# Inverting the triangular blocks of two recurrent layers: to and from the inverter by copies and 32x32 transpositions on chip in place of DRAM transfers

## The chip, the cores and the metric

The kernel runs on one core of a Trainium2 chip. A core has TensorE (PE, matrix products), VectorE (DVE), ScalarE (ACT), GpSimd (POOL) and SyncE (SP), which here issues the DMA transfers. Each engine works through its own queue of instructions in order; engines wait for each other by semaphores. The metric is the device time of one launch in microseconds, as a median over runs.

## The reference

A trunk of four residual layers on one sequence of 256 positions and width 1024, in float32. Layers 0 and 3 mix the positions with RWKV-7, layer 1 with stick-breaking attention, layer 2 with a sparse attention over 64 selected keys; a SwiGLU network follows each. What the change touches is the RWKV mixer, cut to its recurrence:

```python
def step(state, inp):                      # state: 64 x 64 per head, 16 heads
    r_t, w_t, k_t, v_t, kk_t, a_t = inp
    sa = jnp.einsum('bhvk,bhk->bhv', state, kk_t)
    state = (state * w_t[:, :, None, :]
             - sa[..., None] * (kk_t * a_t)[:, :, None, :]
             + v_t[..., None] * k_t[:, :, None, :])
    return state, jnp.einsum('bhvk,bhk->bhv', state, r_t)
_, y = lax.scan(step, s0, (r, decay, k, v, kk, a))
...                                        # norm of y per head, plus (sum r*k*r_k) * v
out = (y * g) @ w_out                      # g: the gate
```

## The kernel before, in words

The 256 positions are cut into four chunks of 64. Within a chunk the recurrence is solved at once: the scores of a chunk form a strictly triangular 64x64 matrix per head, and the inverse of (one plus that matrix) is applied to the chunk's vectors. 16 heads and 4 chunks make 64 such matrices. From chunk to chunk a 64x64 state per head is passed on.

One RWKV layer runs through these steps; the names are those of the profile. Products for keys, values, receptance and gates come first. Then PE makes the scores ("sc"), and DVE multiplies them by a mask into "SB" (16 operations of 128x512 per layer; SB holds the triangular matrices). The 32x32 blocks on the diagonal, two for each of the 64 matrices, lie in four groups of 32 partitions. They are inverted all at once by DVE: the tile "inv" gives each of the 128 blocks a partition of its own, its first half (`ab_`) the block and its second half (`XI`) the inverse, which begins as the identity. 31 steps follow, each of them a product into "xtmp" and a subtraction into "inv"; step i works on (i + 1) rows of (31 − i) elements.

The inverted blocks go to "XT" in the layout that the products want. `combine` then fills XT's off-diagonal blocks, for two of the eight head pairs at a time: DVE transposes XT into "xd", PE makes 32x32 products ("cmb"), which are copied to "zs", PE makes a second set of products, and the result goes to XT. After that the recurrence over the chunks can start: products "pS", "xu", "qu", "Sn" and "Y", each small, each needing what came before it.

How the blocks get from SB to inv and from inv to XT, before: on the chip's DRAM. Eight DMAs write SB's blocks to "scr" in another order of axes, one DMA reads scr into `ab_`, and one loads the identity into `XI`. After the 31 steps one DMA writes `XI` to "scx" and eight DMAs read it back into XT. All are issued on SP's queue, which also loads the weights ("raw").

Meanwhile PE has other work from the same layer that the recurrence does not wait for at once: the value products ("vp", and in layer 3 "pv"), transpositions "qct", "vtok", the products "bv" (SB with the values), the sums "bn" and the gate products "pg". A bn takes its operand from DVE ("prs", split into high and low parts as "prhl", by a CAST and a subtraction), and its result goes through DVE again ("pr"). A pg takes the gate weights' high part "wh" (a cast, on ACT or DVE), low part "wl" (a subtraction on DVE), and the rest of them as "wy" (made on DVE).

The order on each engine is not that of the code. A class `Plan` records all operations, and a list scheduler with its own table of costs and ranks places them on the engines before the program is built; operations of the queue `anye` go to ACT or DVE as it decides. It repeats this 16 times (ROUNDS) and once more with a table `NUDGES`, whose entries shift the ranks of ranges of operations by pseudo-random amounts. Where PE would have nothing to do it puts in dummy bf16 products ("warm_o", L1831 before). All other instructions are emitted from one line (L780 before, L765 after), so the profile's groups are told apart by names. The delay that the scheduler reckons with for a DMA has an extra part, `op.lag`.

Of the kernel before, what the change touches and what calls it, by code (L numbers as in the profile page):

```python
# [28 lines left out]
NCH = S // C  # L29
# [159 lines left out]
class Queue:  # L189
# [152 lines left out]
class Plan:  # L342
# [37 lines left out]
    def record(self, eng, method, args, kw):  # L380
# [22 lines left out]
        if "dma" in method and isinstance(args[0], View):  # L403
            op.lands = args[0].buf.kind == "dram"
            op.lag = 900.0 if args[0].buf.group == "raw" else 0.0
# [378 lines left out]
def trunk(ctx: ExitStack, tc: tile.TileContext, xT_in, vecs_in, wts, lora_in, consts_in, id32_in, nqk_in, outT, order, layers=None):  # L784
# [11 lines left out]
    def T(shape, group=None, name="t", dtype=F32):  # L796
        return plan.tile(sb, [P] + list(shape), dtype, group, name)
# [273 lines left out]
    def rwkv(j, layer, after):  # L1071
# [208 lines left out]
        scr = plan.tile(dram, [4, 32, 32, 32], F32, None, f"scr{j}", "dram")  # L1280
        for g in range(4):
            b = g % 2
            for k in range(2):
                sp.dma_start(scr[g][16 * k:16 * k + 16].rearrange("u i t -> i u t"),
                             SB[k][g * 32:(g + 1) * 32, g // 2, :, :, 0, b * 32:(b + 1) * 32].rearrange("p a c t -> p (a c) t"))
        inv = T([2, 32, 32], "s7", "inv")
        ab_, XI = inv[:, 0], inv[:, 1]
        sp.dma_start(ab_, scr.rearrange("g u i t -> (g u) i t"))
        sp.dma_start(XI, id32_in)
        xtmp = T([S], "xtmp", "xtmp")  # L1290
        for i in range(31):
            t = xtmp[:, :(i + 1) * (31 - i)].rearrange("p (a b) -> p a b", a=i + 1)
            a = ab_[:, i:i + 1, i + 1:].to_broadcast([P, i + 1, 31 - i])
# [700 lines left out]
```

## Time and profile before

| what | us |
|---|---|
| median of three runs (lowest, highest) | 1399.46 (1389.28, 1410.45) |
| the profiled execution, its own time | 1401.71 |
| its span in the trace | 1399.9 |
| PE, DVE, ACT busy in it | 1384.5, 1113.9, 750.4 |
| mean granted clock of PE, share of full | 0.991 |

1.8 us of the profiled execution lie around its span. The profile's times count from the span's start. A row of the timeline or the chain gives the start, the length, the engine, the operation with output<-input, and in brackets the idle time of the engine before it with what ended it; a row for a group gives total busy time and the mean of one in ns. The granted clock is the share of TensorE's full clock that the chip allowed in a window. Rows of ACT and DVE overlap slightly where one instruction starts before the last has drained.

### The profile page before, as it was taken

The numbers are of one execution on the slowest core, as the hardware profiler recorded it, in microseconds if no ns is written. First come the engines' busy times: TensorE is split into PE (matmuls) and PEld (weight loads), VectorE is DVE, ScalarE is ACT, GpSimd is POOL, SyncE is SP. The second block draws the span as 40 slices with busy tenths as digits, with TensorE's granted clock in tenths as the row PEclk, the third lists the DMA queues.
The fourth block names the chain that finished last, engine by engine and source line by source line (L and its number), as shares of the span: only waits on it lengthen the run. The fifth ranks groups of instructions, "written<-read, shape, count | busy, mean of one in ns | idle before, by whom it ended". The sixth has DMA issues, their size and how long they took to land.

```text
span 1399.9 us, 25594 instructions
## 1 busy us (share of the span) xinstructions
PE 1384.5 (99%) x10204; PEld 1195.1 (85%) x10204; DVE 1113.9 (80%) x1960; ACT 750.4 (54%) x1280; POOL 8.0 (1%) x16
## 2 busy tenths in 40 slices
PE   8999999999999999999999999999999999999998
PEld 7888898888888898888887798888878878988887
DVE  7988598887667779896689888986499875988864
ACT  4755675444456755354466864444349256744532
POOL 0000000000000000000000000000000000000000
PEclk9999899999999999999999999999999989999999
DMA  7344155555555355665655445555543440555563
GB/s 254 102 129 140 33 152 184 191 188 189 183 180 158 119 154 192 184 194 183 210 165 151 158 153 181 193 183 189 155 136 110 117 139 20 166 190 186 181 191 126
DMA packets 78231, 224.26 MB, mean 160 GB/s; under 512 B 23712, under 2 KB 24224, under 8 KB 77856
## 3 DMA queue, kind: packets, MB, share of 16 engines
q1 hardware_dynamic: 78112, 222.63, 50.6%
q8 instruction: 80, 1.31, 0.4%
q14 instruction: 39, 0.32, 0.1%
HBM read 219.46 MB, written 3.15 MB: 159 GB/s over the span
## 4 chain that ended last, share of the span: by engine, by line
PE 93%; DVE 3%; DMA 2%; SPq 1%; ACT 0%; issue 0%; DVEq 0%
PE gate L780 18%; PE up L780 18%; PE dn L780 18%; PE po L780 7%; PE rp L780 3%; PE qk L780 3%; PE kp L780 3%; PE vps L780 3%; PE vp L780 2%; PE z L780 2%; PE q L780 2%; PE k L780 2%; PE Y L780 1%; PE sc L780 1%; DMA raw<-in_wts_dram 1%; PE cmb L780 1%
## 5 line engine op out<-in xcount | busy, mean ns | idle before, releaser
L780 ACT CAST wh<-raw 128x1024 fp32r<-128x1024 f32 x329 | 344.6, 1051 | 364.2 <-PE dn L780 112.6
L780 DVE TENSOR_TENSOR wl<-raw,wh 128x1024 fp32r<-128x1024 f32 x375 | 453.2, 1221 | 80.4 <-ACT wh L780 72.9
L780 PE MATMUL up<-xg,wh 128*128 128x512 f32 x704 | 255.3, 397 | 0.0
L780 PE MATMUL gate<-xg,wh 128*128 128x512 f32 x704 | 254.3, 396 | 0.0
L780 PE MATMUL dn<-h,wh 128*128 128x512 f32 x704 | 247.1, 395 | 0.0
L780 PE MATMUL up<-xg,wl 128*128 128x256 f32 x704 | 197.5, 280 | 0.0
L780 PE MATMUL gate<-xg,wl 128*128 128x256 f32 x704 | 197.4, 280 | 0.0
L780 PE MATMUL dn<-h,wl 128*128 128x256 f32 x704 | 197.2, 280 | 0.0
L780 PEld LDWEIGHTS gate<-xg,wh 128*128 128x128 f32 x704 | 132.0, 188 | 31.2
L780 PEld LDWEIGHTS up<-xg,wh 128*128 128x128 f32 x704 | 132.0, 188 | 31.0
L780 PEld LDWEIGHTS dn<-h,wh 128*128 128x128 f32 x704 | 132.0, 188 | 30.9
L780 PEld LDWEIGHTS up<-xg,wl 128*128 128x128 f32 x704 | 133.0, 189 | 0.2
L780 PEld LDWEIGHTS gate<-xg,wl 128*128 128x128 f32 x704 | 133.0, 189 | 0.1
L780 PEld LDWEIGHTS dn<-h,wl 128*128 128x128 f32 x704 | 133.0, 189 | 0.0
L780 DVE TENSOR_TENSOR gus<-gus,rstd 128x512 f32<-128x512 f32 x88 | 59.6, 686 | 0.8
L780 PE MATMUL vp<-xv,raw 128*128 128x256 f32 x256 | 58.3, 384 | 0.0
L780 PEld LDWEIGHTS vp<-xv,raw 128*128 128x128 f32 x256 | 47.6, 190 | 8.0 <-issue 0.7
L780 PE MATMUL rp<-prx,wh 128*128 128x256 f32 x256 | 51.2, 299 | 0.0
L780 DVE TENSOR_TENSOR xt<-xt,dn 128x256 f32<-128x256 f32 x64 | 26.8, 418 | 30.3 <-PE dn L780 29.7
L780 PE MATMUL po<-yhl,wh 128*128 128x256 f32 x256 | 49.4, 293 | 0.0
L780 PE MATMUL po<-ohl,wh 128*128 128x256 f32 x256 | 48.4, 289 | 0.0
L780 PE MATMUL qk<-xg,wh 128*128 128x512 f32 x128 | 46.4, 403 | 0.0
(318 smaller groups left out, 2385.0 us busy)
## 6 DMA issues: line engine op xcount, KB each, us to landing
raw<-in_wts_dram SPq DMA_DIRECT2D x401, 512.0 KB, 3.7
lora<-in_lora_dram SPq DMA_DIRECT2D x2, 1280.0 KB, 9.8
xt<-in_xT_dram SPq DMA_DIRECT2D x4, 256.0 KB, 3.7
lora<-in_lora_dram SPq DMA_DIRECT2D x2, 512.0 KB, 6.2
scr<-SB SPq DMA_DIRECT2D x16, 64.0 KB, 1.9
inv<-in_id_dram SPq DMA_DIRECT2D x2, 512.0 KB, 3.7
inv<-scr SPq DMA_DIRECT2D x2, 512.0 KB, 4.6
scx<-inv SPq DMA_DIRECT2D x2, 512.0 KB, 3.4
```

Source lines behind the costliest of these rows:

```text
L780: getattr(getattr(nc, o.eng), method)(*map(real, args), **{k: real(a) for k, a in kw.items()})
```

## The change

Four edits.

One: the way in. Eight copies (queue `anye`, 32 partitions x 512 elements each) put SB's blocks into a tile "blocks" with axes [row t, k, a, c], and one DVE transposition of all 32x32 blocks, 128x1024, writes `inv[:, 0]`. The identity is still loaded by DMA. Two: because a 32x32 transposition leaves the axes of a partition the other way round, the views `ab_` and `XI` on inv are rearranged from [i, t] storage to [t, i] storage: what was the inner axis of a step's operands, one float from the next, now goes 32 floats from one element to the next, and what was the outer axis is now contiguous. The 31 steps are otherwise the same. Three: the way out. A second transposition of 128x1024 goes from `inv[:, 1]` to another "blocks" tile, and eight copies from there fill XT. The 18 DMAs per layer through scr and scx are gone. Four: `op.lag` becomes 2500 for a DMA into a part of a tile on chip that is not contiguous (900 remains for "raw"), and NUDGES is a new table; both change the order of the whole program.

```diff
 NUDGES = [[
-    (424148, 5631, 5681, 1000), (179145, 5680, 5980, 1000), (140712, 6286, 6406, 1000), (48283, 6712, 6762, 8000),
...
+    (441210, 581, 589, 3000), (474839, 1087, 1387, 1000), (64567, 1455, 1505, 300), (132794, 641, 649, 1000),
...
-            op.lag = 900.0 if args[0].buf.group == "raw" else 0.0
+            wide = not op.lands and args[0].region().mask is not None
+            op.lag = 900.0 if args[0].buf.group == "raw" else 2500.0 if wide else 0.0
...
-        scr = plan.tile(dram, [4, 32, 32, 32], F32, None, f"scr{j}", "dram")
-        for g in range(4):
-            b = g % 2
-            for k in range(2):
-                sp.dma_start(scr[g][16 * k:16 * k + 16].rearrange("u i t -> i u t"),
-                             SB[k][g * 32:(g + 1) * 32, g // 2, :, :, 0, b * 32:(b + 1) * 32].rearrange("p a c t -> p (a c) t"))
+        ct_ = T([32, 2, 4, NCH], "blocks", "blocks")
+        for k in range(2):
+            for g in range(4):
+                r, b = slice(g * 32, (g + 1) * 32), g % 2
+                anye.copy(ct_[r, :, k].rearrange("p t a c -> p a c t"), SB[k][r, g // 2, :, :, 0, b * 32:(b + 1) * 32])
         inv = T([2, 32, 32], "s7", "inv")
-        ab_, XI = inv[:, 0], inv[:, 1]
-        sp.dma_start(ab_, scr.rearrange("g u i t -> (g u) i t"))
-        sp.dma_start(XI, id32_in)
+        dve.transpose(flat(inv[:, 0]), ct_.rearrange("p t k a c -> p (t k a c)"))
+        sp.dma_start(inv[:, 1], id32_in)
+        ab_, XI = [inv[:, i].rearrange("p t i -> p i t") for i in range(2)]
         xtmp = T([S], "xtmp", "xtmp")
         for i in range(31):
             t = xtmp[:, :(i + 1) * (31 - i)].rearrange("p (a b) -> p a b", a=i + 1)
             a = ab_[:, i:i + 1, i + 1:].to_broadcast([P, i + 1, 31 - i])
             b = XI[:, :i + 1, i:i + 1].to_broadcast([P, i + 1, 31 - i])
             dve.tensor_tensor(t, a, b, op=ALU.mult)
             dve.tensor_tensor(XI[:, :i + 1, i + 1:], XI[:, :i + 1, i + 1:], t, op=ALU.subtract)
-        scx = plan.tile(dram, [4, 32, 32, 32], F32, None, f"scx{j}", "dram")
-
         XT = [T([16, C], t, "XT") for t in ("wh", "wl")]
         for k in range(2):
             anye.memset(XT[k], 0.0)
-        sp.dma_start(scx.rearrange("g u i t -> (g u) i t"), XI)
+        ct_ = T([32, 2, 16], "blocks", "blocks")
+        dve.transpose(ct_.rearrange("p t k u -> p (t k u)"), flat(inv[:, 1]))
         for k in range(2):
             for g in range(4):
-                b = g % 2
-                sp.dma_start(XT[k][g * 32:(g + 1) * 32, :, b * 32:(b + 1) * 32],
-                             scx[g][16 * k:16 * k + 16].rearrange("u i t -> i u t"))
+                r, b = slice(g * 32, (g + 1) * 32), g % 2
+                anye.copy(XT[k][r, :, b * 32:(b + 1) * 32], ct_[r, :, k].rearrange("p t u -> p u t"))
```

Three places show how the order moved. The first is DVE's queue in layer 0 where the scores end, before the change: the last mask products and what is put ahead of the wait for the DMA chain (names as above; a trailing x and number is how many in a row).

```order
L780 TENSOR_TENSOR SB<-sc,consts_91 128x512 x4
L780 TENSOR_TENSOR pr<-PR,QC 128x512
L780 TENSOR_TENSOR SB<-sc,consts_91 128x512 x4
L780 TENSOR_TENSOR pr<-PR,QC 128x512 x3
```

And the same place after the change, up to the first step of the inversion.

```order
L765 TENSOR_TENSOR SB<-sc,consts_91 128x512 x5
L765 COPY blocks<-SB 32x16x32
L765 TENSOR_TENSOR pr<-PR,QC 128x512
L765 TENSOR_TENSOR SB<-sc,consts_91 128x512 x4
L765 TENSOR_TENSOR pr<-PR,QC 128x512
L765 COPY blocks<-SB 32x16x32
L765 TENSOR_TENSOR pr<-PR,QC 128x512
L765 STREAM_TRANSPOSE inv<-blocks 128x1024
L765 TENSOR_TENSOR pr<-PR,QC 128x512
L765 TENSOR_TENSOR xtmp<-inv 128x31
```

Two of the eight block copies stand on DVE here, six on ACT, and the transposition stands between two pr operations directly ahead of the first step.

The second place is DVE's queue in layer 0 at the end of the inversion, before the change.

```order
L780 TENSOR_TENSOR inv<-inv,xtmp 128x31
L780 TENSOR_TENSOR wy<-raw_1205,wy 32x1024
L780 TENSOR_TENSOR wl_1450<-raw_1177,wh_1199 128x1024
L780 TENSOR_TENSOR pr<-bn,vf_111 128x512
L780 TENSOR_TENSOR prhl<-prs,prhl 128x512
L780 TENSOR_TENSOR pr<-bn,vf_112 128x512
L780 CAST prhl<-prs 128x512
L780 TENSOR_TENSOR prhl<-prs,prhl 128x512
L780 TENSOR_TENSOR pr<-bn,vf_113 128x512
L780 TENSOR_TENSOR pr<-bn,vf_114 128x512
L780 STREAM_TRANSPOSE xd<-XT 128x512 x4
```

The same place after the change.

```order
L765 TENSOR_TENSOR wy<-raw_1210,wy 32x1024
L765 TENSOR_TENSOR inv<-inv,xtmp 128x29x3
L765 TENSOR_TENSOR wl_1374<-raw_1186,wh_1207 128x1024
L765 TENSOR_TENSOR xtmp<-inv 128x60
L765 TENSOR_TENSOR inv<-inv,xtmp 128x30x2
L765 TENSOR_TENSOR xtmp<-inv 128x31
L765 TENSOR_TENSOR inv<-inv,xtmp 128x31
L765 COPY QC<-qct 128x8x64
L765 STREAM_TRANSPOSE blocks<-inv 128x1024
L765 COPY XT<-blocks 32x16x32 x4
L765 CAST prhl<-prs 128x512
L765 TENSOR_TENSOR pr<-bn,vf_112 128x512
```

wy and wl stand between the last steps now and no longer behind them; four of the eight XT copies are on DVE (four on ACT) ahead of the CAST for the third bn. Behind these rows come `prhl`, the first `xd` and a `pr`.

The third place is PE's queue in layer 0 ahead of the first combination, before the change: the last bn and the gate products.

```order
L780 MATMUL bn<-prhl,bonesr 128x512 x2
L780 MATMUL pg<-gx,wh_1199 128x256 x2
L780 MATMUL pg<-gx,wl_1450 128x256
L780 MATMUL pg<-gy,wy 128x256
L780 MATMUL pg<-gx,wh_1199 128x256 x2
L780 MATMUL pg<-gx,wl_1450 128x256
L780 MATMUL pg<-gy,wy 128x256
```

Two more such triples of pg follow there, and then 32 cmb. After the change the place reads as follows.

```order
L765 MATMUL pg<-gy,wy 128x256
L765 MATMUL bn<-prhl,bonesr 128x512 x2
L765 MATMUL bv<-UV,SB 64x64 x16
L765 MATMUL cmb_1544<-xd,SB 32x32 x16
L765 MATMUL pg<-gx,wh_1207 128x256 x2
L765 MATMUL pg<-gx,wl_1374 128x256
L765 MATMUL pg<-gy,wy 128x256
L765 MATMUL bn<-prhl,bonesr 128x512 x2
L765 MATMUL pg<-gx,wh_1207 128x256 x2
L765 MATMUL pg<-gx,wl_1374 128x256
```

The bn ahead of cmb is the third of four here, and the fourth bn with most of the gate products stands behind the first 16 cmb, among the recurrence's products. The dummies in the order go from 142 to 124, with 12 instead of 22 in layer 0's recurrence and 14 instead of 26 in layer 3's.

88 rows, old and new, of the table NUDGES are left out of this document.

## The prediction

> **What bounds the kernel now.** I read first the page's head and its chain of waits by engine, then the busy time by stage, then the chain, the DVE timeline and the PE timeline around the two inversions.
>
> ```profile
> span 1399.9 us, 25594 instructions
> PE 1384.5 (99%) x10204; PEld 1195.1 (85%) x10204; DVE 1113.9 (80%) x1960; ACT 750.4 (54%) x1280; POOL 8.0 (1%) x16
> PE 93%; DVE 3%; DMA 2%; SPq 1%; ACT 0%; issue 0%; DVEq 0%
> ```
>
> TensorE (PE) is busy 1384.5 of 1399.9 us and holds 93% of the chain; DVE, DMA and SPq share the 6% on which this change can act. The next two rows are the recurrent layers, layer 0 and layer 3 (columns: window, its length, then busy us of PE, PEld, DVE, ACT, POOL, the granted clock, DMA share, GB/s).
>
> ```profile
> 0.00:198.00 198.00, 191.47 (x2167) 165.42 (x2168) 157.60 (x334) 118.89 (x243) 4.41 (x10) 0.97 0.43 133
> 1010.00:1210.00 200.00, 195.59 (x2181) 166.23 (x2182) 163.53 (x335) 118.77 (x243) 2.61 (x3) 0.97 0.36 105
> ```
>
> PE idles 198 − 191.47 = 6.5 us in the first and 4.4 in the second, 10.9 of the kernel's 15.4; in the first some is start-up. Idle alone is small, but the clock is below 1. The chain of waits shows layer 0's route from scores to recurrence (start, length, what):
>
> ```profile
> 94.75 1.93 DMA scr<-SB
> 96.89 4.58 DMA inv<-scr
> ...
> 125.42 1.22 DVE wy L780
> 126.67 1.24 DVE wl L780
> ...
> 129.91 5.14 DMA XT<-scx
> 135.17 0.72 DVE xd L780
> ```
>
> Between the second and third of them lie the 62 steps of the inversion. The DVE timeline dates them, layer 0 first, then layer 3 (bracket: idle before, and what ended it):
>
> ```profile
> 90.99 1.89 DVE L780 TENSOR_TENSOR SB<-sc,consts 128x512 f32<-128x512 f32 x3 [0.20 <-PE sc L780]
> 101.57 0.19 DVE L780 TENSOR_TENSOR xtmp<-inv 128x31 f32<-128x31 f32 x1 [4.26 <-DMA inv<-scr]
> 125.17 0.22 DVE L780 TENSOR_TENSOR inv<-inv,xtmp 128x31 f32<-128x31 f32 x1
> 1093.00 2.71 DVE L780 TENSOR_TENSOR SB<-sc,consts 128x512 f32<-128x512 f32 x4
> 1104.33 0.19 DVE L780 TENSOR_TENSOR xtmp<-inv 128x31 f32<-128x31 f32 x1 [0.35 <-DMA inv<-scr]
> 1132.39 0.22 DVE L780 TENSOR_TENSOR inv<-inv,xtmp 128x31 f32<-128x31 f32 x1
> ```
>
> Last score block ready to first step: 101.57 − 92.88 = 8.7 us, and 1104.33 − 1095.71 = 8.6. First to last step: 23.8 and 28.3. What PE does meanwhile is in its timeline:
>
> ```profile
> 127.95 0.39 PE L780 MATMUL pg<-gx,wl 128*128 128x256 f32 x1 [0.73 <-DVE wl L780]
> ...
> 128.86 2.13 PE L780 MATMUL bv<-UV,SB 64*64 64x64 f32 x64
> 130.92 0.73 PE L780 MATMUL bn<-prhl,bonesr 128*128 128x512 f32 x2
> ...
> 133.98 0.40 PE L780 MATMUL pg<-gx,wh 128*128 128x256 f32 x2
> ...
> 134.34 0.28 PE L780 MATMUL pg<-gy,wy 96*128 96x256 f32 x1
> 135.93 1.49 PE L780 MATMUL cmb<-xd,SB 32*32 32x32 f32 x64 [1.32 <-DVE xd L780]
> 1143.77 1.80 PE L780 MATMUL cmb<-xd,SB 32*32 32x32 f32 x64 [1.92 <-DVE xd L780]
> ```
>
> The first combination ("cmb") starts 10.5 us after the last step in layer 0 and 11.2 in layer 3, yet PE idles only 0.73 + 1.32 and 1.92 there: filler (values, sums, gates) covers the route. So removing 8.7 + 10.5 us of route cannot give that back by itself. Its worth is in when PE enters the recurrence, which is a chain of small dependent products with dummy products ("warm_o") in its gaps:
>
> ```profile
> 138.00:146.00 8.00, 8.00 (x136) 5.88 (x136) 4.83 (x8) 3.81 (x12) 0.00 (x0) 0.50 0.25 73
> 1144.00:1156.00 12.00, 12.00 (x211) 9.27 (x207) 5.43 (x8) 6.34 (x16) 0.00 (x0) 0.50 0.37 121
> 120.00:160.00 40.00, 5.36 (x22) 0.87 0.34 95
> 1120.00:1164.00 44.00, 6.28 (x26) 0.84 0.38 112
> ```
>
> After each idle the granted clock is 0.50: the mean of 0.87 over 40 us is 40 × 0.13 / 0.5 = 10.4 us at half speed, and 0.84 over 44 is 14.1. At most half of each, 5.2 and 7.0 us, is lost to it. The last two rows' busy time is the dummies alone, 11.6 us in both layers. A recurrence that starts earlier, or work that replaces dummies, draws on these sums.
>
> **The change, part by part.** The way in. The eight block copies and the transposition replace nine DMAs. Rows for the new operations:
>
> ```profile
> L780 DVE TENSOR_TENSOR wl<-raw,wh 128x1024 fp32r<-128x1024 f32 x375 | 453.2, 1221 | 80.4 <-ACT wh L780 72.9 <-PE po L780 2.5
> L780 DVE STREAM_TRANSPOSE xd<-XT 128x512 f32<-128x512 f32 x8 | 5.2, 690 | 5.4 <-DMA XT<-scx 5.4
> L780 DVE COPY QC<-QC 128x512 f32<-128x512 f32 x1 | 0.4, 425 | 0.0
> L780 ACT COPY QC<-QC 128x512 f32<-128x512 f32 x7 | 4.3, 618 | 4.0 <-DVE QC L780 4.0
> 95.50 0.69 DVE L780 TENSOR_TENSOR prhl<-prs,prhl 128x512 fp32r<-128x512 f32 x1
> ```
>
> A 128x1024 transposition is between 1.22 (an elementwise operation of that size) and 1.38 (two of 512); I take 1.22. A copy of 512 elements is 0.43 on DVE, 0.62 on ACT. After the last score block, DVE's order (above, under the change) in layer 0 has a pr, a copy, a pr, the transposition and a pr. A pr is worth 0.60 (three took 1.89, overlapping): 3 × 0.60 + 0.43 to 0.69 + 1.22 gives 3.5, so the first step is at about 96.4 instead of 101.6: **−5.2**. Layer 3 has two copies, a pr, the transposition and a pr: about 3.3, so 1099.0, **−5.3**. ACT's copies lie in time in which it waits and cost nothing; if that cover is gone, one 0.62 shows. The SP queue is rid of 36 transfers; the brackets above name DVE and not a weight load as what PE waited for, so zero.
>
> The steps. Their element counts are as before, Σ(i+1)(31−i) = 5456 for each of the two kinds, 10,912 a layer. But the inner walk now goes 32 floats, 128 bytes, at a time through `inv`. Before, it did so only in the very last step, where each row holds one element. First step, last step, and the two neighbours with 60 elements:
>
> ```profile
> L780 DVE TENSOR_TENSOR xtmp<-inv 128x31 f32<-128x31 f32 x1 | 0.2, 193 | 4.3 <-DMA inv<-scr 4.3
> L780 DVE TENSOR_TENSOR inv<-inv,xtmp 128x31 f32<-128x31 f32 x1 | 0.2, 192 | 0.0
> ...
> L780 DVE TENSOR_TENSOR inv<-inv,xtmp 128x31 f32<-128x31 f32 x1 | 0.2, 216 | 0.0
> L780 DVE TENSOR_TENSOR xtmp<-inv 128x31 f32<-128x31 f32 x1 | 0.2, 211 | 0.0
> ...
> L780 DVE TENSOR_TENSOR xtmp<-inv 128x256 f32<-128x256 f32 x1 | 0.4, 424 | 0.0
> 102.02 0.22 DVE L780 TENSOR_TENSOR xtmp<-inv 128x60 f32<-128x60 f32 x1
> 124.41 0.22 DVE L780 TENSOR_TENSOR xtmp<-inv 128x60 f32<-128x60 f32 x1
> ```
>
> The same 31 elements cost 18 ns (mul) and 24 ns (sub) more when each lies 128 bytes from the next; 60 elements in pairs (30 rows of 2) cost no more than 2 rows of 30. Per element 18/31 = 0.58 and 24/31 = 0.77 ns, so 5456 × (0.58 + 0.77) = **+7.4 us a layer**. The lower end takes the excess as fixed per instruction: 62 × 21 ns = +1.3. The upper end takes a second full slot per element, (424 − 193)/225 = 1.03 ns: +11.2. [...]
>
> [...]
>
> The way out. DVE, after the last step in layer 0: copy QC 0.6, transposition 1.22, four XT copies 1.7 to 2.8, then CAST 0.33, pr 0.6 and prhl 0.6 ahead of the first xd. This is 5 to 6 us where before 9.8 passed (125.4 to 135.17). Work of others put between the steps: in layer 0 wy and wl (2.45 together), two prhl (0.6 each) and four small ones that partly fit the gaps, 3.9 in all, against 0.6 before; in layer 3 the 10 operations of before made 28.3 − 23.3 = 5.0, half a us each, and 21 make about 10.8.
>
> Sums without the stride: layer 0, 96.4 + 23.3 of steps + 3.9 = 123.6; + 6 to 7.2, and a xd: first cmb 130 to 132, against 135.93, **−4 to −6**. Layer 3: 1099.0 + 23.3 + 10.8 = 1133.1, first cmb 1138 to 1139, against 1143.77, **−5 to −6**. With +9.4: 139 to 141 and 1147 to 1148.5: **about +4 in each layer**.
>
> What then waits. PE's order now keeps two bn pairs, 16 bv and five pg triples (two weights' halves and wy, one after the other) behind the wait in layer 0: the third bn needs the prhl that DVE makes after its XT copies. Before, seven pg triples and the bns stood ahead of cmb, and PE ran dry only 1.3 us before it. After, PE's in-order queue stops at the first wl, then at the third bn: with the stride some 10 us go by with 1.4 us of work of its own. What is held back (five pg triples, one running from 133.98 to about 134.5, so 0.5 each; two bn pairs of 0.6; 16 bv, a quarter of the 2.13; some 4 us) is not lost: it lies in the recurrence where dummies stood (22 of 5.36 us before; 12 in the order now). That gives back 0 to 2 us a layer. PE idles long enough that the half clock comes again, as before. Changed order elsewhere I take at ±3: outside the two stages PE idles 15.4 − 10.9 = 4.5 us in all.
>
> **Forecast:** 2 × 4 = 8, less 0 to 4 by replaced dummies: **+4**. From the profiled run's 1401.7 that is 1405.7; that run is 2.2 above the median shown, so **1404**, own range 1396 to 1414.
>
> **The rivals.** (1) The stride is free, and the change does what it removes: each layer's cmb comes 5.5 us earlier. PE still idles about 4.6 us a layer (it reaches the third bn near 126 to 129), yet enters the recurrence with 4 us of filler and is spared part of the half-clock time: −2 × 5.5, and half of 5.2 + 7.0 = 6.1 more, −17 with ±6: **1382**. For it: the 60-element rows show no excess, and the 31-element excess may be a fixed one. Against: 18 and 24 ns in the only rows with this walk. [...]
> (2) The excess is partly there, +4 to +6 a layer: cmb stays where it was, dummies make room: −8 to 0, **1396**.
> (3) Slower: the in-order wait at the third bn. If cmb comes 8 or more us later than before (stride at its upper end, XT copies on DVE at their upper end), PE is dry long enough that the clock stays at half through the filler and the start of the recurrence; 25 us more at half in each layer cost 12.5 each, with 2 × 6 of shift: about +35, **1434**. It decides where PE's idle in the stage goes beyond some 10 us; for it, the 10.4 and 14.1 us at half follow only 2.0 and 1.9 us of idle; against, both ran back to full speed in the middle of the recurrence.
>
> **How the numbers follow.** Forecast 0.59, rival 1 0.23, rival 2 0.11, rival 3 0.07. 2% is 28 us (1371.5 and 1427.4), about what can be told from no change here. Rival 1 reaches beyond 1371.5 only at its far end: faster 0.04; rival 3 gives slower 0.06; same 0.90. The runs before spread from 1389 to 1410 on one kernel, so the range goes from rival 1's middle less 5, 1377, to 1419, five above the forecast's own end; it leaves out rival 3 and rival 1's far half, some 0.18.
>
> **What would show it.** Right: the long steps (xtmp and inv of 256) at 0.57 to 0.69 us instead of 0.42, the last ones unchanged near 0.21; first step near 96 and 1099; the last near 133 and 1142; the first cmb near 140 and 1148; PE idle before the first pg with wl and before the third bn, some 5 us each; half clock after it. Wrong: long steps still at 0.42, and cmb at 131 and 1139 (rival 1); a mean clock under 0.95 in the two stages' windows (rival 3); or PE work outside these stages that moved by more than 3 us, which would mean that the new order, not the route, made the time.

## The result, and the profile after

| | before | after |
|---|---|---|
| median, us (runs) | 1396.01 (19) | 1404.32 (19) |
| lowest to highest | 1389.28 to 1410.45 | 1400.74 to 1406.58 |
| profiled execution, its span | 1401.71, 1399.9 | 1405.27, 1403.5 |

The ratio of after to before is 1.0058, 95% interval 1.0045 to 1.0072: the changed kernel is slower by 0.6%, within the 2% that was called no change. (Ratios compare undisturbed runs and need not be the quotient of the medians.) The runs of before spread over 21 us, those of after over 6, and the two profiled executions are only 3.6 apart. Why will be seen.

The page's head and its chain by engine, after:

```profile
span 1403.5 us, 25541 instructions
PE 1379.8 (98%) x10186; PEld 1193.3 (85%) x10186; DVE 1139.0 (81%) x1979; ACT 770.9 (55%) x1296; POOL 9.8 (1%) x17
PE 89%; DVE 9%; DMA 1%; ACT 1%; issue 1%; SPq 0%; DVEq 0%
```

In the chain PE lost 4 points and DVE took 6. The work by stage says where (columns as in the prediction; layer 0 ends near 202 here, layer 3 runs from about 1015):

```profile
0.00:202.00 202.00, 190.85 (x2165) 165.89 (x2165) 170.92 (x344) 129.51 (x251) 5.12 (x10) 0.98 0.37 120
1015.00:1215.00 200.00, 191.66 (x2168) 164.73 (x2167) 175.81 (x343) 126.88 (x254) 3.85 (x3) 0.97 0.30 94
```

PE idles 11.2 us in layer 0 (6.5 before) and 8.3 in layer 3 (4.4 before). The DVE timeline, layer 0, from the last scores to the first combination:

```profile
91.61 2.53 DVE L765 TENSOR_TENSOR SB<-sc,consts 128x512 f32<-128x512 f32 x4
...
96.52 1.25 DVE L765 STREAM_TRANSPOSE inv<-blocks 128x1024 f32<-128x1024 f32 x1 [0.42 <-ACT blocks L765]
...
98.26 0.19 DVE L765 TENSOR_TENSOR xtmp<-inv 128x31 f32<-128x31 f32 x1
...
115.60 0.63 DVE L765 TENSOR_TENSOR inv<-inv,xtmp 128x256 f32<-128x256 f32 x1
...
132.90 0.19 DVE L765 TENSOR_TENSOR inv<-inv,xtmp 128x31 f32<-128x31 f32 x1
133.01 0.68 DVE L765 COPY QC<-qct 128x512 f32<-128x512 f32 x1
133.61 1.23 DVE L765 STREAM_TRANSPOSE blocks<-inv 128x1024 f32<-128x1024 f32 x1
134.94 2.46 DVE L765 COPY XT<-blocks 32x512 f32<-32x512 f32 x4
```

From the last score block (94.14) to the first step are 4.1 us, not 8.7: the route in is shorter, as it should be. But a step of 256 elements takes 0.63 us where it took 0.42, and the inversion ends at 133.1, not at 125.4. The sum of the steps in each layer, before (first fence) and after (second), windows that hold all 62 of a layer (here the columns are DVE busy, granted clock, DMA share, GB/s):

```profile
96.00:136.00 40.00, 21.25 (x62) 1.00 0.57 171
1100.00:1148.00 48.00, 21.18 (x62) 0.96 0.47 142
```

```profile
96.00:136.00 40.00, 28.75 (x62) 0.93 0.43 132
1100.00:1148.00 48.00, 28.60 (x62) 0.89 0.35 110
```

**+7.5 and +7.4 us a layer** for the same elements. PE's timeline after, layer 0 and then layer 3:

```profile
133.84 1.97 PE L765 MATMUL bv<-UV,SB 64*64 64x64 f32 x32 [7.71 <-DVE QC L765]
...
140.62 0.69 PE L765 MATMUL cmb<-xd,SB 32*32 32x32 f32 x32
...
1118.54 3.75 PE L765 MATMUL vp<-xv,raw 128*128 128x256 f32 x8 [2.55 <-issue]
...
1144.11 3.49 PE L765 MATMUL vtok<-consts,vf 64*64 64x64 f32 x64 [2.80 <-DVE vf L765]
...
1152.43 0.69 PE L765 MATMUL cmb<-xd,SB 32*32 32x32 f32 x32
```

PE waits 7.71 us in layer 0 for a copy ("QC", which empties a bank of "qct"; the "bv" that waits draws its bank from the same pool) that stands in DVE's queue behind the last step, and 2.80 us in layer 3 for a value sum ("vf") that stands between the steps. For the 2.55 us ahead of "vp" in layer 3 the profile names no releaser; another such value sum ended on DVE at 1118.44, 0.1 us before, so the cause is probably the same, but this is not shown. The first cmb is 4.7 us later in layer 0; in layer 3 it is 8.7 later, of which 5.5 had come before the layer began. The clock, after (windows of four us and one of twenty, columns as in the stage rows):

```profile
132.00:136.00 4.00, 2.16 (x33) 2.08 (x34) 3.78 (x9) 1.06 (x1) 0.00 (x0) 0.50 0.75 249
136.00:140.00 4.00, 4.00 (x32) 3.16 (x34) 3.94 (x8) 3.28 (x6) 0.00 (x0) 0.89 0.01 2
140.00:160.00 20.00, 19.88 (x530) 16.60 (x528) 12.17 (x29) 15.44 (x41) 0.00 (x0) 1.00 0.18 57
```

The half clock falls in the wait and in the first products behind it, and is over when the recurrence begins. In layer 3 it is the same: the mean clock is 0.57 from 1116 to 1124, around the wait of 2.55 us, 0.50 from 1144 to 1146, behind the wait of 2.80, and 1.00 from 1148 on. Before, it lay on the recurrence itself.

### The profile page after: what moved, and what is told of

It reads as the page before. It is cut to its first block, busy times and chain, and to the rows that moved or that the text cites. A ratio compares the mean times of both kernels' runs of the same rounds, so it can differ in the third digit from the quotient of the medians.

```text
span 1403.5 us, 25541 instructions
## 1 busy us (share of the span) xinstructions
PE 1379.8 (98%) x10186; PEld 1193.3 (85%) x10186; DVE 1139.0 (81%) x1979; ACT 770.9 (55%) x1296; POOL 9.8 (1%) x17
## 4 chain that ended last, share of the span: by engine, by line
PE 89%; DVE 9%; DMA 1%; ACT 1%; issue 1%; SPq 0%; DVEq 0%
PE up L765 18%; PE dn L765 18%; PE gate L765 18%; PE po L765 7%; PE qk L765 3%; PE vps L765 3%; PE rp L765 3%; PE kp L765 2%; DVE inv L765 2%; PE z L765 2%; DVE xtmp L765 2%; PE q L765 2%; PE k L765 2%; PE Y L765 1%; PE attn_o L765 1%; PE qi L765 1%
## 5 line engine op out<-in xcount | busy, mean ns | idle before, releaser
L765 ACT CAST wh<-raw 128x1024 fp32r<-128x1024 f32 x336 | 351.6, 1050 | 381.9 <-PE dn L765 111.4
L765 PEld LDWEIGHTS dn<-h,wl 128*128 128x128 f32 x704 | 133.1, 189 | 0.0
```

What stands on the lines that cost most here:

```text
L765: getattr(getattr(nc, o.eng), method)(*map(real, args), **{k: real(a) for k, a in kw.items()})
```

## The experiments

Two theories. **Stride**: the steps are slower because the inner walk goes 128 bytes at a time, they lie on the path to cmb, and that is what eats the shorter route. **Order**: PE's stops come from where the new order puts copies and sums, and the steps' length matters little. Seven runs were made.

**The walk made contiguous, on the changed kernel.** The same outer product is run with its axes exchanged; PE's, ACT's and SP's orders and DVE's are as in the changed kernel, step for step.

```diff
-        ab_, XI = [inv[:, i].rearrange("p t i -> p i t") for i in range(2)]
+        ab_, XI = inv[:, 0], inv[:, 1]
...
-            t = xtmp[:, :(i + 1) * (31 - i)].rearrange("p (a b) -> p a b", a=i + 1)
-            a = ab_[:, i:i + 1, i + 1:].to_broadcast([P, i + 1, 31 - i])
-            b = XI[:, :i + 1, i:i + 1].to_broadcast([P, i + 1, 31 - i])
+            t = xtmp[:, :(i + 1) * (31 - i)].rearrange("p (b a) -> p b a", a=i + 1)
+            a = ab_[:, i + 1:, i:i + 1].to_broadcast([P, 31 - i, i + 1])
+            b = XI[:, i:i + 1, :i + 1].to_broadcast([P, 31 - i, i + 1])
             dve.tensor_tensor(t, a, b, op=ALU.mult)
-            dve.tensor_tensor(XI[:, :i + 1, i + 1:], XI[:, :i + 1, i + 1:], t, op=ALU.subtract)
+            dve.tensor_tensor(XI[:, i + 1:, :i + 1], XI[:, i + 1:, :i + 1], t, op=ALU.subtract)
```

> The changed kernel with the two axes of each inversion step exchanged, so that the inner walk through inv is one float from the next again; same element counts, same order on every engine. Theory (the stride is on the path): steps of 256 elements back from about 0.61 to 0.42 us, the steps of a layer back from 28.7 to about 21.2 us; last step of layer 0 near 125.5 instead of 133.1, so PE's wait of 7.7 us at bv goes, with the half clock behind it; first cmb near 132.5 instead of 140.6; in layer 3 PE's wait of 2.8 us at vtok goes. Time 1404 less 12, 1388 to 1396. Rival (PE's stops come from where DVE's queue puts the copies and sums, and the recurrence takes up any shift): first cmb less than 3 us earlier, time 1401 to 1407.

Measured: 1388.59 (1387.82 to 1389.78, 7 runs), 15.7 below the changed kernel, and 0.9941 of before (0.992 to 0.9962): it is the fastest of the three, though by less than 2%. Its timeline of PE:

```profile
125.44 1.15 PE L765 MATMUL bv<-UV,SB 64*64 64x64 f32 x32 [0.21 <-DVE QC L765]
...
130.29 1.00 PE L765 MATMUL bn<-prhl,bonesr 128*128 128x512 f32 x2 [1.16 <-DVE pr L765]
...
132.30 0.69 PE L765 MATMUL cmb<-xd,SB 32*32 32x32 f32 x32
```

The steps of a layer take 21.20 and 21.09 us again. The wait of 7.71 us is 0.21, cmb is at 132.3, and what is left is a wait ahead of the third bn, where the prediction had put one, 1.16 (for a pr, by the profile). In layer 3 the waits of 2.55 and 2.80 us are gone, and cmb starts 123.1 us behind the layer's first key product (kp) instead of 130.5. The order theory falls: with the order untouched, the steps' length alone moves 15.7 us. Between the two traces, the stretch from the first score to the first product of the SwiGLU network is shorter by 7.6 us in layer 0 and by 7.2 in layer 3, about the 7.5 and 7.4 by which the steps had grown. The clock stands at full where layer 0's recurrence starts:

```profile
120.00:160.00 40.00, 38.59 (x921) 31.84 (x918) 28.07 (x66) 32.63 (x77) 0.00 (x0) 1.00 0.22 70
```

The time is at the lower end of what the stride theory gave.

**The walk made strided, on the kernel before.** The same exchange the other way round; route and order as before.

```diff
-            t = xtmp[:, :(i + 1) * (31 - i)].rearrange("p (a b) -> p a b", a=i + 1)
+            t = xtmp[:, :(i + 1) * (31 - i)].rearrange("p (b a) -> p b a", a=i + 1)
...
-            dve.tensor_tensor(XI[:, :i + 1, i + 1:], XI[:, :i + 1, i + 1:], t, op=ALU.subtract)
+            dve.tensor_tensor(*[XI[:, :i + 1, i + 1:].rearrange("p r t -> p t r")] * 2, t, op=ALU.subtract)
```

(The operands a and b are turned in the same way.)

> The kernel before, route through DRAM and order unchanged, with only the two axes of each step exchanged so that the inner walk goes 128 bytes at a time. Theory: steps of a layer from 21.2 to 28.7 us, first cmb in each layer 7 to 7.5 us later than before, and since nothing stands ready to fill that time PE idles about 9 us in each of the two layers; time 1396 plus 12 to 18. Rival (the inversion is not what sets the first cmb; the transfers and the gate products are): the steps longer, but the time within 4 of before.

Measured: 1412.96 (1404.88 to 1416.52, 5 runs), 17 above the 1395.93 of before; ratio 1.0104 (1.0067 to 1.014). PE's waits in it, layer 0 and layer 3:

```profile
129.56 3.68 PE L780 MATMUL bv<-UV,SB 64*64 64x64 f32 x64 [6.34 <-DVE QC L780]
...
144.40 1.38 PE L780 MATMUL cmb<-xd,SB 32*32 32x32 f32 x64 [1.57 <-DVE xd L780]
...
1149.26 1.97 PE L780 MATMUL vtok<-consts,vf 64*64 64x64 f32 x32 [5.40 <-DVE vf L780]
```

The steps take 28.85 and 28.98 us, as expected. cmb is 8.5 us later than the 135.93 of before, a little more than the expected 7 to 7.5; in layer 3 it is 7.4 later, counted from the layer's first key product. PE's waits above 0.5 us around the inversion come to 8.5 us in layer 0 and 6.8 in layer 3, where about 9 were expected. The stride costs about the same in either kernel, 15.7 and 17 us, and here too PE stops first not at cmb but at a small copy and a value sum that DVE makes behind or between the steps.

**The price of a stride by itself.** A program of single operations on 128 x 256 floats, with the spacing from one element to the next varied. Its core, for VectorE:

```python
nc.vector.tensor_tensor(d, step(src, s), flat_, op=ALU.mult)            # read at spacing s
nc.vector.tensor_tensor(step(d, s), flat_, flat_, op=ALU.mult)          # written
nc.vector.tensor_tensor(step(d, s), step(d, s), flat_, op=ALU.mult)     # read and written
```

> Not the trunk: a program of single operations on 128 partitions x 256 floats, each with its operand read, written, or read and written at 4, 8, 12, 16, 32, 64 and 128 bytes from one element to the next, on VectorE (product of two tensors) and ScalarE (copy), and in pairs of neighbours 128 bytes apart. It computes no part of the reference. [...] Rival (the price grows with the distance or lies in the write): a slope from 16 to 128 bytes, or a written stride at 580 or more.

Groups of that program (the name gives the spacing in bytes; "rd" read, "w" written, "w<-w" both; then the pairs of neighbours; ScalarE's copies in the second fence, "ca" read):

```profile
L40 DVE TENSOR_TENSOR rd8B<-big,flat 128x256 f32<-128x256 f32 x2 | 0.8, 418 | 0.0
L40 DVE TENSOR_TENSOR rd12B<-big,flat 128x256 f32<-128x256 f32 x2 | 1.0, 492 | 0.0
L40 DVE TENSOR_TENSOR rd16B<-big,flat 128x256 f32<-128x256 f32 x2 | 1.2, 596 | 0.0
L40 DVE TENSOR_TENSOR rd128B<-big,flat 128x256 f32<-128x256 f32 x2 | 1.2, 606 | 0.0
L42 DVE TENSOR_TENSOR w16B<-flat 128x256 f32<-128x256 f32 x2 | 1.2, 611 | 0.0
L42 DVE TENSOR_TENSOR w128B<-flat 128x256 f32<-128x256 f32 x2 | 1.2, 625 | 0.0
L44 DVE TENSOR_TENSOR w128B<-w128B,flat 128x256 f32<-128x256 f32 x2 | 1.3, 654 | 0.1
L51 DVE TENSOR_TENSOR pairrd<-big,flat 128x256 f32<-128x256 f32 x2 | 0.9, 426 | 0.0
```

```profile
L46 ACT COPY ca4B<-big 128x256 f32<-128x256 f32 x2 | 0.8, 402 | 7.4 <-DVE big L23 7.4
L46 ACT COPY ca128B<-big 128x256 f32<-128x256 f32 x2 | 1.3, 646 | 0.0
```

Against 422 ns for a read at 4 bytes, one at 8 cost nothing more (418), at 12 a part (492), at 16 the whole (596), and at 128 about as much (606); pairs of neighbours cost nothing more (426). Why the price sets in between 8 and 16 bytes is not shown. The rival was right in one of its two points: a written stride cost as much as a read one, 611 at 16 bytes and 625 at 128, and both together, 654 at 128, hardly more than one. A price that grows from 16 to 128 bytes did not come. ScalarE pays as well, 646 ns at 128 bytes against 402 at 4. Per element of VectorE the price is (606 − 422) / 256 = 0.72 ns (422 at 4 bytes), which times 10,912 elements is 7.8 us; 7.5 was measured in the kernel. (Half of the steps read and write `inv` at the stride. By the row that does both, 654 against 425 ns, they would cost 0.89 ns an element and the sum would be 8.8, so the estimate is good to about 1 us.)

**A second trace of the kernel before.**

> The kernel before, unchanged, for another trace of it: its profiled execution took 1401.7 where the median of its runs is 1396.0. Theory: the difference is in how long PE's clock stays at half around the two first combinations or in waits for transfers of that route, so this trace has either a time near 1396 with less half clock or less idle in the two layers. Rival: the difference is spread over the whole program.

Measured: 1398.18. It met its expectation in layer 3 only. There the wait ahead of cmb is shorter, and the clock stays up (PE timeline, then the window that stood at 0.50 in the first trace):

```profile
1145.73 1.20 PE L780 MATMUL cmb<-xd,SB 32*32 32x32 f32 x64 [0.41 <-DVE xd L780]
```

```profile
1144.00:1156.00 12.00, 11.59 (x302) 9.42 (x300) 7.59 (x14) 8.53 (x24) 0.00 (x0) 1.00 0.51 147
```

302 products in the window instead of 211. Against the first trace layer 3 gains 7.1 us, and other places lose 3.6. In layer 0 it was the other way: PE waited 2.24 us ahead of cmb instead of 1.32, and the clock over 120 to 160 was 0.83 instead of 0.87. So in these two traces a wait of 0.41 us ahead of cmb left the clock at 1.00, and waits of 1.32 to 2.24 were followed by one of 0.50. From the last step to cmb, the stretch in which the transfers run, 10.5 and 11.2 us passed in the first trace and 11.5 and 9.8 in the second: the kernel before draws a lot each time. That the landing of its transfers decides it is the author's guess and was not shown.

**The wait ahead of cmb filled with dummies, on the kernel before.** 14 more dummy products ahead of the first cmb of each layer.

```diff
+            if o.eng == "tensor" and o.instrs[0][1][0].buf.name == "cmb1" and o.idx - last > 1000:
+                last = o.idx
+                [warmer() for _ in range(7)]
```

> The kernel before with 14 more dummy products on PE directly ahead of the first cmb of each recurrent layer, where PE stood idle for 0.6 to 2.4 us; nothing else differs. Theory (the idle ahead of cmb brings the half clock, and the half clock is what makes the runs before spread from 1390 to 1402): the granted clock stays near 1.0 through both recurrences, mean clock 0.998 or more, runs within 5 of each other, median 1389 to 1392 instead of 1396. Rival (the small products of the recurrence themselves bring the half clock): clock at 0.5 there as before, median 1394 to 1398.

Measured: 1392.89 (1390.27 to 1393.55, 12 runs) against 1396.97 for before on that chip; ratio 0.9964 (0.9939 to 0.999). Mean clock 0.999 to 1.0 in all of its runs, where those of before had 0.985 to 1.0 with times from 1410.9 to 1389.9. Its windows over both recurrences (dummies alone; columns: PE busy, clock, DMA share, GB/s):

```profile
120.00:160.00 40.00, 5.33 (x36) 1.00 0.34 95
1120.00:1164.00 44.00, 6.28 (x40) 1.00 0.37 110
```

The half clock is gone and with it the spread. The rival is out: the recurrence's small products ran at a clock of 1.00 in both windows, with PE idle for 0.06 us ahead of the first cmb of layer 0. (That a wait must come first is not shown for other small products, as the last section says.) The median is 1 us above the expected 1389 to 1392; the dummies may delay cmb where the data come early.

**Without the table.** Before and the contiguous version, both with the table emptied, so that neither has a tuned order.

```diff
-NUDGES = [[ ... ]]
+NUDGES = []
```

> The kernel before with its table NUDGES emptied, so that the scheduler's own order stands. It is one half of a pair with the next. Theory (the route and the walk make the difference between the kernels, the table little): 1396 to 1412, and slower than its partner by 5 to 12. Rival (the new table makes it): the two of the pair within 3 of each other.

> The route on chip with the contiguous walk and the new rule for the delay of transfers, with the table emptied: the other half of the pair. Theory: 1390 to 1402, 5 to 12 below its partner, first cmb 3 to 4 us earlier in each layer. Rival (the gain of 7 over the kernel before is the new table's): within 3 of its partner.

Measured: 1414.32 (1412.64 to 1416.19, 4 runs) and 1409.44 (1404.89 to 1415.43, 10 runs). Both times missed: 1396 to 1412 and 1390 to 1402 had been expected, so the tables were worth more than thought. The two are 4.9 apart, just under the expected 5 to 12, with overlapping ranges. The first cmb is 1.9 us earlier in layer 0 and 7.1 in layer 3 in their traces (1.7 of it from before the layer), where 3 to 4 in each were expected. Each table is worth about 20 us to its kernel (1414 to 1396, 1409 to 1389), and the two kernels differ by 4.9 without tables and 7.4 with them. The gain is thus more likely the route's than the table's, but with this spread the pair does not settle it.

## Why the prediction was right, and where not

**The result** lies at the forecast, 1404.32 against 1404. The mechanism was right, but that the time was met so closely is luck: two misses cancelled in it. By its own steps it reads as follows.

**The way in, −5.2 and −5.3: right in kind.** From the last score block to the first step 4.1 us instead of 8.7 in layer 0, −4.6. In layer 3 the first step follows 3.65 us after the last block (1101.40 to 1105.05), −5.0. The two transpositions took 1.25 and 1.23 us, for 1.22 assumed.

**The steps, +9.4 taken: the mechanism right, the size at its lower reading.** No run shows the 9.4 that the sums use: 7.5 and 7.4 were measured, and the per-element price from the 31-element rows gave +7.4. The choice towards the upper end was the author's estimate and the mistake: those rows had 0.58 and 0.77 ns an element, and the 62 steps of a layer together 7.5 us over 10,912 elements, 0.69. That the price lies in both kinds of step about alike was in the rows already.

**Rival 1, the free stride, is out,** by the 0.63 us of a step and by both exchanges. Its time for a free stride, 1382, can be set against the contiguous version: 1388.6. It gave −5.5 for the first cmb and half of the half clock; cmb came 3.6 earlier in layer 0 (132.30 against 135.93), and 4.2 in layer 3 (from the layer's first key product), and the base was too high, as below. Against the median of before the contiguous version gains 7.4. The three runs of before beside it on the same chip whose mean clock was 1.0 took 1389.95, 1391.16 and 1391.94. As an estimate from these, about 3 of the 7.4 are the route's and the order's own, and the rest is the clock's.

**The first cmb, about +4 in each layer: right.** It came 4.7 later in layer 0, of which 1.3 had come before the last scores, so 3.4 from this part; and 8.7 − 5.5 = 3.2 in layer 3. Here too misses made up for each other: the steps cost 1.9 and 2.0 less than taken, and the rest brought cmb forward by 4.1 and 4.2, at the low end of the 4 to 6 and below the 5 to 6 that were reckoned.

**Where PE waits: the wrong place.** The prediction had PE stop at the first wl and at the third bn. It stopped earlier, at a bv that waits for the QC copy behind the last step, and in layer 3 at a vtok that waits for a value sum between the steps. The QC copy was in the row quoted from DVE's order; I counted its 0.6 us and did not ask who waits for it. The idle time was 7.7 us in layer 0 where some 10 were forecast, and 2.80 and 2.55 in layer 3.

**The half clock comes again: right, but in another place.** Because PE ran dry earlier, the half clock fell on the wait and on bv and bn. The recurrence ran at full clock (1.00 from 140 to 160 and from 1148 to 1176) and took back 1.1 us in layer 0 and 3.2 in layer 3 of the shift, counted to the first product of the network behind. The prediction gave that part to dummies replaced by filler, 0 to 2 a layer; their share was not separated from the clock's.

**The sum, +4, and its base.** Between the two profiled executions +3.6 was measured: +3.6 by the end of layer 0 (0.6 of it from the start-up), nothing in layer 3 after the 3.2 were taken back, and +1.9 and −1.9 in between and behind. Between the medians it is +8.3. The step that failed is the base: the profiled run of before had the half clock in layer 3, which with the longer wait there cost it 7.1 us against the second trace, and I subtracted only 2.2 for it, from three runs whose median lay 3.4 above that of nineteen. So the sum set the changed kernel against a long execution of the kernel before: the step +4 was too small by 4.3, the base of 1399.5 too high by 3.5, and the forecast time was right because the two nearly cancel.

**Rival 2** (a part of the excess) and **rival 3** (the clock at half through the recurrence) did not come. Rival 3 asked for more than some 10 us of idle in the stage and a cmb 8 us later or more. PE idled 11.2 us in layer 0's window, 7.7 of them in the one wait, but cmb came only 4.7 later, and the clock was back at full before 140.

**The signs.** The long steps at 0.62 and 0.63 us and the last ones at 0.19 came as said. In layer 0 the first step (98.3), the last (132.9) and cmb (140.6) lie within 2.3 us of what was said; in layer 3 they came 4 to 6 us later than said, after everything had moved by 5.5 before the layer began. The wait ahead of the first pg with wl did not come.

## What to carry to other kernels

A change of layout can move cost into the later operations that walk the data: here copies and two transpositions of 1.2 us brought the first cmb some 4 us forward in each layer, and made 62 small operations dearer by 7.5 us, and exchanging the two axes of those operations removed it. Look in the trace for the one row of the old kernel in which the new walk already occurs, and read its price per element without rounding it up. Take the base of a forecast from several executions, and where their granted clocks differ, look first for a short wait ahead of a stretch of small products; here one of 1.32 to 2.24 us was followed by a clock of 0.50, and one of 0.41 was not.

## What the runs showed of the hardware that was not expected

The price of a written stride was not expected: 0.74 to 0.79 ns an element from 16 bytes on (611 to 625 ns for 256 elements, against 422), about that of a read one (582 to 614 ns).

A wait of PE of 1.92 us in layer 3 of the kernel before, with the half clock that followed, cost 7.1 us against the second trace, where one of 0.41 left the clock at 1.00. Ahead of the larger products of a bn, one of 1.16 in the contiguous version left it at 1.00 as well (120 to 164), and so did 1.46 us of idle in all over the same window of the filled one. The length of the half clock did not follow that of the wait. From 120 to 164 the mean clock was 0.88 in the kernel before, whose wait ahead of the first cmb was 1.32 us, and 0.84 in its second trace, with 2.24, but 0.92 in the changed kernel, with the wait of 7.71. And in layer 3 of the contiguous version the clock fell (0.65 from 1104 to 1108, 0.93 from 1108 to 1112) behind small products, with 0.49 us of idle of PE in all from 1100 to 1112. What decides the half clock is thus only in part shown.

The feed-forward stages ran at one of two paces, with a clock of 1.00 in both, and the same program drew one in one run and the other in the next. These are PE's products in the same 90 us of the second feed-forward stage of the kernel before, in its first trace and in its second:

```profile
530.00:620.00 90.00, 90.00 (x521) 1.00 0.61 192
```

```profile
530.00:620.00 90.00, 90.00 (x511) 1.00 0.58 187
```

521 against 511 products is 2%. From the start times of the products, 48 of them take 8.48, 8.32, 8.32 and 8.48 us in the median of the four stages in the first trace of the kernel before, and 8.48, 8.48, 8.32 and 8.32 in that of the changed kernel. In the former the two stages at 8.32 took 185.9 and 185.1 us from first product to last, those at 8.48 took 187.3 and 186.8. What decides it was not found.
